# Order of the first loads, half-size V chunks, unnormed pool projection, paired FFN units and another buffer for y in an eight-core trunk kernel

## The chip, the cores and the metric

One Trainium2 chip; the program runs on all eight cores, each with its own rows and the same weights. The metric is the device time of the slowest core in microseconds (us). A run is called *slow* when one die (cores 0 to 3, or 4 to 7) is over 1% longer than the other at a lower clock of TensorE (PE), or when the run is over 1.5% above the fastest of its kernel. Only *fast* runs are compared.

## The reference

Each core carries 2048 prompt rows and 64 sample rows through four layers, in two groups `g` of 1024 prompt rows (the first with the sample rows). A layer is a token mixer and a gated FFN; even layers mix by gMLP, odd ones by pooling.

```python
for i in range(4):
    h = rmsnorm(x, norm_mix[i])
    if i % 2 == 0:                       # gMLP
        u, v = split(gelu(h @ w_in))     # 2048 columns each
        v = rmsnorm(v, g_v)              # per row, over 2048 columns
        y = (u * (masked_ws @ v + b_s)) @ w_out
    else:                                # pooling: trailing means over 2, 4, 8, 16 rows
        y = grouped(mean(h) - h, w_pool) * scale
    x = x + y
    h = rmsnorm(x, norm_ffn[i])
    x = x + (silu(causal_conv3(h @ w_gate)) * (h @ w_val)) @ w_down
y = rmsnorm(x, norm_final)
```

## The kernel before

The kernel records operations with the buffers that they read and write; a scheduler at build time then lays out one fixed order for each engine. So a load that the program text names first need not be first in its engine's queue. Weights come in 1 MB units through a ring of 64 KB per partition, issued by POOL (GpSimd); x, y and some of the constants are issued by SP (SyncE). DVE is VectorE, and PSUM the memory that matmuls write to, here handed out in banks of 512 columns. A group's rows are three tiles of up to 384.

```python
load_x(0, 0)                       # tile 0, two halves, SP
unit(("Uu", 0, 0, 0))              # first weight unit, POOL
...
for t in range(1, 3):
    load_x(0, t)                   # not gated by anything

# gMLP, V: one f32 buffer for a chunk of 128 rows x 2048 columns
for ci, (col0, nt, t) in enumerate(chunks):
    for half in range(2):
        ...                        # 16 matmuls into two PSUM banks
        rec(ACT, ... out=vsb.t[0:nt, half * 1024:(half + 1) * 1024] ... Gelu ...)
    rec(ACT, ... Square of all of vsb, sum into vs ...)
    rsqrt_col(vs, nt)              # twelve one-column operations, DVE
    rec(DVE, ... vb = vsb * rsqrt * g_v, 2048 columns ...)
    ...                            # spatial product: bias row, 16 matmuls from vb

# FFN
for u in range(6):
    wg = unit(("Wg", g, l, u)); wv = unit(("Wv", g, l, u))
    for t, (c0, n) in enumerate(TILES[g]):
        ...                        # gate and value matmuls, 4 pairs (u = 5: 2)

# end of a group
def final_tile(g, t):
    ...                            # DVE: xT = xT * scale * rstd, in place
    dma(SP, y_out ..., xT ...)     # two halves
# and then load_x(g + 1, t) into the same xT
```

Before a pooling layer all rows were normed (Ln and Exp on ScalarE, eight scalings on DVE), then projected, 1024 columns at a time over two PSUM banks.

Of the kernel before, what the change touches and what calls it, by code (L numbers as in the profile page):

```python
# [16 lines left out]
DV = 2048  # L17
# [101 lines left out]
class Recorder:  # L119
# [3 lines left out]
    def rec(self, eng, fn, reads=(), writes=(), cost=0.0, dsem=None, nbytes=0, tab=None, pt=()):  # L123
# [21 lines left out]
        for w in writes:  # L145
            for o in w.overl:
                if o.last_write is not None:
                    add(o.last_write, False)
                for t in o.reads:
                    add(t, False)  # L150
        deps.pop(op, None)
# [11 lines left out]
    def schedule(self, engines, window=160):  # L163
# [16 lines left out]
        dma_free = [0.0]  # L180
# [18 lines left out]
        def best(name):  # L199
# [8 lines left out]
            while i < L and n < window:  # L208
# [9 lines left out]
                if op.news:  # L218
                    (tile,) = op.news
                    if tile.pred is not None and tile.pred.b is None:  # L220
                        continue
                    p = place(tile, s, reserved)
                    if p is None:
                        for g_ in tile.groups:
                            reserved.update(g_)
                        continue
                    _, grp, t = p
                    if t > s:
                        reserved.update(grp)
                        s = t  # L230
# [8 lines left out]
        while remaining:  # L239
# [35 lines left out]
            if op.dsem is not None:  # L275
                b = max(s + c + 1.3, dma_free[0])
                dma_free[0] = b + op.nbytes / 230e3
                op.end = dma_free[0] + 0.8
            else:
                op.end = s + c  # L280
# [58 lines left out]
def build_program():  # L339
# [44 lines left out]
    with es:  # L384
# [42 lines left out]
        for i in range(2):  # L427
            vnb.append(alloc(f"vn{i}", [128, DV], BF16, off=o))
            o += 4096
        junk = alloc("junk", [128, DV], BF16, off=o)  # L430
# [9 lines left out]
        hS = alloc("hS", [128, KC, NSM], F32, off=M0 + 4 * NTMAX * 2, pieces=[((k,), k * NSM, (k + 1) * NSM) for k in range(KC)])  # L440
# [26 lines left out]
        vstat = [alloc(f"vstat{i}", [128, 8], F32) for i in range(2)]  # L467
        epsb = alloc("epsb", [128, 1], F32)
# [3 lines left out]
        vsb = alloc("vsb", [128, DV], F32, off=X0 + 8192, pieces=[(0, 0, 1024), (1, 1024, 2048)])  # L472
# [9 lines left out]
        gout = alloc("gout", [64, DV], F32, off=acc[0].off)  # L482
# [44 lines left out]
        def dma(eng, out, in_, reads=(), writes=(), dsem=None, nbytes=0, cost=None):  # L527
            if cost is None:
                cost = 0.9 if eng is POOL else 0.1
            return rec(eng, lambda e: e.dma_start(out=out, in_=in_), reads, writes, cost, dsem, nbytes)  # L530
# [15 lines left out]
        def load_unit(key):  # L546
# [5 lines left out]
            dma(POOL, buf.t[:, :, :].rearrange("p a b -> p (a b)"), sap, writes=buf.all, dsem=ring_sems[i % NRS], nbytes=128 * a * b * 4)  # L552
# [6 lines left out]
        def load_x(g, t):  # L559
            c0, n = TILES[g][t]  # L560
            o = xoff[(g, t)]
            src = x_in[128 * o:128 * (o + KC * n)].rearrange("(p k c) -> p k c", p=128, k=KC)
            for h in range(2):
                ks = slice(4 * h, 4 * h + 4)
                dma(SP, xT.t[:, ks, c0:c0 + n], src[:, ks, :], writes=[xT.r[(k, t)] for k in range(4 * h, 4 * h + 4)],
                    dsem=xsem[(t, h)], nbytes=128 * 4 * n * 4)
# [5 lines left out]
        def const_load(buf, out, src, eng=POOL):  # L572
            cs[id(buf)] = newdsem(f"d_c{len(cs)}")
            dma(eng, out, src, writes=buf.all, dsem=cs[id(buf)], nbytes=100000)

        load_x(0, 0)
        unit(("Uu", 0, 0, 0))
# [6 lines left out]
        def consts_late():  # L584
            const_load(pvf, pvf.t[:, :, :].rearrange("p a b -> p (a b)"), vec_f, SP)
            const_load(maskT, maskT.t[:], c_mask)
# [5 lines left out]
            od = newdsem("d_old")  # L592
            for j in range(2):
                dma(SP, pool_old[j], st_old[j], dsem=newdsem(f"d_old{j}"), nbytes=700000)
# [66 lines left out]
        def norm_pool_extra(g, t, l):  # L661
            c0, n = TILES[g][t]
            rs = rstd[t % 2]
            j = l // 2
            if t != 2:
                return
            if g == 0:
                for kc in range(KC):
                    rec(DVE, lambda e: e.scalar_tensor_tensor(out=hS.t[:, kc, :], in0=xT.t[:, kc, NP:NP + NSM],
                                                               scalar=pvd.t[:, kc, l:l + 1], in1=rs.t[:, 256:320], op0=ALU.mult, op1=ALU.mult),  # L670
                        reads=[xT.r[(kc, t)]] + rs.all + pvd.all, writes=[hS.r[(kc,)]], cost=dvec(NSM, True))
# [3 lines left out]
            else:  # L675
                for kc in range(KC):
                    rec(DVE, lambda e: e.scalar_tensor_tensor(out=hpp.t[:, kc, :], in0=xT.t[:, kc, NP - 15:NP],
                                                               scalar=pvd.t[:, kc, l:l + 1], in1=rs.t[:, 241:256], op0=ALU.mult, op1=ALU.mult),
                        reads=[xT.r[(kc, t)]] + rs.all + pvd.all, writes=hpp.all, cost=dvec(16, True))
                dma(SP, pool_prompt[j], hpp.t[:, :, :].rearrange("p a b -> p (a b)"), reads=hpp.all, dsem=hpp_sem, nbytes=62000)  # L680

        def proj_tile(g, t, mm_list):
            c0, n = TILES[g][t]
            for dc in range(KC):
# [3 lines left out]
                def f(e):  # L688
# [5 lines left out]
                    pt=[(bk, False)], reads=[xT.r[(dc, t)]], writes=[xT.r[(dc, t)]], cost=dvec(n))  # L694
                stat_add(g, t, dc)

        def rsqrt_col(vs, nt):
            def tiny(f):
                rec(DVE, f, reads=vs.all, writes=vs.all, cost=0.13)
            c = lambda i: vs.t[0:nt, i:i + 1]  # L700
            ci_ = lambda i: vs.t[0:nt, i:i + 1].bitcast(I32)
            tiny(lambda e: e.tensor_scalar(out=c(2), in0=c(0), scalar1=EPS, scalar2=None, op0=ALU.add))  # L702
            tiny(lambda e: e.tensor_scalar(out=ci_(3), in0=ci_(2), scalar1=1, scalar2=None, op0=ALU.logical_shift_right))
            tiny(lambda e: e.tensor_scalar(out=ci_(1), in0=ci_(3), scalar1=-1.0, scalar2=1597463007.0, op0=ALU.mult, op1=ALU.add))
            for _ in range(3):
                tiny(lambda e: e.scalar_tensor_tensor(out=c(4), in0=c(1), scalar=c(1), in1=c(2), op0=ALU.mult, op1=ALU.mult))
                tiny(lambda e: e.tensor_scalar(out=c(4), in0=c(4), scalar1=-0.5, scalar2=1.5, op0=ALU.mult, op1=ALU.add))
                tiny(lambda e: e.tensor_tensor(out=c(1), in0=c(1), in1=c(4), op=ALU.mult))
# [5 lines left out]
        def mixer_a(g, l, after_tile):  # L714
            j = l // 2
            dma(SP, gvb.t[:], g_v[j].partition_broadcast(128), writes=gvb.all, dsem=gv_sem, nbytes=1048576)
# [13 lines left out]
            for t, (c0, n) in enumerate(TILES[g]):  # L730
                for u in range(4):
# [17 lines left out]
            for ci, (col0, nt, t) in enumerate(chunks):  # L749
                vb = vnb[ci % 2]  # L750
                vs = vstat[ci % 2]
                for half in range(2):
                    bks = palloc(2, range(4), chain='v')

                    def mmv(e):
                        for q in range(2):
                            w = vu[2 * half + q]
                            for kc in range(KC):
# [5 lines left out]
                    rec(ACT, lambda e: e.activation(out=vsb.t[0:nt, half * 1024:(half + 1) * 1024], in_=pap(bks, 0, 1024)[0:nt, :], func=AF.Gelu_apprx_tanh),  # L764
                        pt=[(bks, False)], writes=[vsb.r[half]], cost=actc(1024), tab="gelu")
                rec(ACT, lambda e: e.activation(out=junk.t[0:nt, :], in_=vsb.t[0:nt, :], func=AF.Square, scale=float(DV) ** -0.5, accum_out=vs.t[0:nt, 0:1]),  # L766
                    reads=vsb.all, writes=junk.all + vs.all, cost=actc(2048) + 0.2)
                rsqrt_col(vs, nt)
                rec(DVE, lambda e: e.scalar_tensor_tensor(out=vb.t[0:nt, :], in0=vsb.t[0:nt, :], scalar=vs.t[0:nt, 1:2], in1=gvb.t[0:nt, :],  # L769
                                                          op0=ALU.mult, op1=ALU.mult),  # L770
                    reads=vsb.all + vs.all + gvb.all, writes=vb.all, cost=dvec(2048, True))
                if nt == NSM:
                    rec(DVE, lambda e: e.scalar_tensor_tensor(out=gout.t[:], in0=vsb.t[0:NSM, :], scalar=vs.t[0:NSM, 1:2], in1=gvb.t[0:NSM, :],
                                                              op0=ALU.mult, op1=ALU.mult),
                        reads=vsb.all + vs.all + gvb.all, writes=gout.all, cost=dvec(2048, True))
# [51 lines left out]
        def mixer_b_tile(g, l, t):  # L827
# [3 lines left out]
            for t, (c0, n) in [(t, TILES[g][t])]:  # L831
                cl = [c for c in range(8) if c // 3 == t]
                for c in cl:
                    zt = zb[c] if not (g == 0 and c == 7) else zlast[j]
                    ztile[c] = zt
                    bks = palloc(2)

                    def mmz(e):
                        for gi in range(4):
                            for cc in range(2):  # L840
                                i = e.matmul(pap(bks, gi * 256, (gi + 1) * 256), lhsT=hB.t[:, 2 * gi + cc, 2 + c * 128:2 + (c + 1) * 128],  # L841
                                             rhs=wp.t[:, 2 * gi + cc, :], start=(cc == 0), stop=(cc == 1))
                        return i
                    rec(PE, mmz, reads=wp.all + [hB.r[(kc, t)] for kc in range(KC)], pt=[(bks, True)], cost=mmc(8, 256))
# [339 lines left out]
```

## Time and profile before

| what | before |
|---|---|
| all runs, median | 3122.05 us (20 runs, 3052.05 to 3446.16) |
| PE busy, slowest core | 2895.5 us of 3078.8 |
| PE clock, mean of the cores | 0.945 to 0.966 |
| DVE, ScalarE (ACT), POOL busy | 49%, 39%, 15% |

The PE is the bound, so the kernel's time is its matmul work plus what it idles plus what it loses by running below full clock. The list of cores is the view to start from; its columns are span and mean clock:

```profile
core 0: 3052.7 us, clock 0.953
...
core 4: 3023.0 us, clock 0.965
core 5: 3015.3 us, clock 0.966
...
core 7: 3078.8 us, clock 0.945
```

Same program, same instructions, 64 us apart, and the longer the span, the lower the clock, but for cores 1 to 3, which lie within 4 us. Where this trace shows a clock of 0.8125, it lasts 159.5 to 161.5 us at a time: once on cores 0 to 3, twice on 6 and 7, never on 4 and 5. In the first of core 7 (629 to 791 us) matmuls of 384 columns start 197 ns apart, where they start 162 ns apart at clock 1.00 (800 to 900 us). Each costs 161 x (1 - 0.8125) = 30 us. Below I call these *0.81 stretches*, and take them out of stage lengths, since they hide what a change does.

### The profile page before, as it was taken

The numbers are of one execution on the slowest core, as the hardware profiler recorded it, in microseconds if no ns is written. First come the engines' busy times: TensorE is split into PE (matmuls) and PEld (weight loads), VectorE is DVE, ScalarE is ACT, GpSimd is POOL, SyncE is SP. The second block draws the span as 40 slices with busy tenths as digits, with TensorE's granted clock in tenths as the row PEclk, the third lists the DMA queues.
The fourth block names the chain that finished last, engine by engine and source line by source line (L and its number), as shares of the span: only waits on it lengthen the run. The fifth ranks groups of instructions, "written<-read, shape, count | busy, mean of one in ns | idle before, by whom it ended". The sixth has DMA issues, their size and how long they took to land.

```text
span 3078.8 us, 51559 instructions; the slowest of 8 cores (3015.3 to 3078.8 us)
## 1 busy us (share of the span) xinstructions
PE 2895.5 (94%) x18552; PEld 1806.7 (59%) x18552; DVE 1516.1 (49%) x2968; ACT 1186.0 (39%) x2209; POOL 471.4 (15%) x832
## 2 busy tenths in 40 slices
PE   1989999899999999989998999999999999999998
PEld 0545666555664566655565556666666556666665
DVE  1056663455314666355533356635663166635663
ACT  1433442533243344244324434424443334424541
POOL 1003221112210222212121021010002011011001
PEclk8999999888999999988899999998999999998999
DMA  9407441543344563263437435324453434424341
GB/s 190 73 6 124 67 73 33 91 65 57 56 72 66 96 94 49 45 104 60 63 80 158 69 59 98 56 41 83 70 97 65 80 55 83 71 41 84 58 74 55
DMA packets 49272, 227.76 MB, mean 74 GB/s; under 512 B 6240, under 2 KB 19168, under 8 KB 31456
## 3 DMA queue, kind: packets, MB, share of 16 engines
q0 software_dynamic: 32960, 193.75, 39.1%
q1 hardware_dynamic: 16064, 30.72, 3.4%
q8 instruction: 153, 2.51, 0.3%
q14 instruction: 95, 0.78, 0.1%
HBM read 406.32 MB, written 13.32 MB: 136 GB/s over the span
## 4 chain that ended last, share of the span: by engine, by line
PE 82%; DVE 7%; ACT 4%; issue 3%; DMA 3%; another core or an unknown queue 1%; DVEq 0%; SPq 0%; ACTq 0%
PE psum L690 26%; PE psum L923 22%; PE psum L930 21%; PE psum L739 7%; PE psum L888 2%; PE psum L759 2%; ACT junk L766 1%; DMA xT<-x_in 1%; DMA y_out<-xT 1%; DVE hB L653 1%; DVE vn_48 L769 1%; DVE vn_47 L769 1%; PE psum L841 1%; ACT vsb L764 1%
## 5 line engine op out<-in xcount | busy, mean ns | idle before, releaser
L693 DVE TENSOR_TENSOR xT<-psum,xT 128x384 f32<-128x384 f32 (+2 forms) x288 | 147.9, 522 | 483.5 <-PE psum L690 483.1
L947 DVE SCALAR_TENSOR_TENSOR cb_91<-psum,pvf,cb_91 128x384 f32<-128x384 f32 (+1 forms) x264 | 151.0, 572 | 68.7 <-ACT cb_91 L937 42.4
L947 DVE SCALAR_TENSOR_TENSOR cb_90<-psum,pvf,cb_90 128x384 f32<-128x384 f32 (+1 forms) x264 | 150.7, 571 | 65.6 <-ACT cb_90 L937 52.5
L947 DVE SCALAR_TENSOR_TENSOR cb_89<-psum,pvf,cb_89 128x384 f32<-128x384 f32 (+1 forms) x264 | 150.8, 571 | 63.1 <-ACT cb_89 L937 39.4
L947 DVE SCALAR_TENSOR_TENSOR cb_88<-psum,pvf,cb_88 128x384 f32<-128x384 f32 (+1 forms) x264 | 150.8, 571 | 55.7 <-ACT cb_88 L937 44.1
L602 ACT ACTIVATE sq_58<-xT 128x384 f32<-128x384 f32 (+2 forms) x126 | 62.4, 496 | 283.1 <-DVE xT L693 263.4
L602 ACT ACTIVATE sq_57<-xT 128x384 f32<-128x384 f32 (+2 forms) x126 | 62.4, 495 | 280.2 <-DVE xT L693 258.9
L653 DVE SCALAR_TENSOR_TENSOR hB<-xT,pvd,rstd_64 128x384 bf16<-128x384 f32 (+2 forms) x256 | 129.9, 579 | 67.1 <-ACT rstd_64 L645 67.1
L764 ACT ACTIVATE vsb<-psum 128x1024 f32<-128x1024 f32 (+1 forms) x68 | 66.4, 1021 | 230.8 <-DVE vn_47 L769 94.1
L743 ACT ACTIVATE UB<-psum 128x384 bf16<-128x384 f32 (+2 forms) x192 | 86.4, 466 | 108.4 <-PE psum L739 108.1
L937 ACT ACTIVATE cb_90<-psum,pvf 128x384 f32<-128x384 f32 (+2 forms) x132 | 84.4, 639 | 112.5 <-PE psum L923 110.1
L937 ACT ACTIVATE cb_88<-psum,pvf 128x384 f32<-128x384 f32 x132 | 84.5, 640 | 105.5 <-PE psum L923 103.4
L937 ACT ACTIVATE cb_91<-psum,pvf 128x384 f32<-128x384 f32 (+2 forms) x132 | 84.3, 639 | 101.6 <-PE psum L923 101.6
L937 ACT ACTIVATE cb_89<-psum,pvf 128x384 f32<-128x384 f32 x132 | 84.2, 638 | 91.0 <-PE psum L923 91.0
L702 DVE TENSOR_SCALAR vstat_81<-vstat_81 128x1 f32<-128x1 f32 (+1 forms) x18 | 2.7, 152 | 226.0 <-ACT junk L766 226.0
L954 POOL TENSOR_SCALAR stmp_84<-ASb,pvf 128x64 f32<-128x64 f32 x88 | 38.8, 440 | 479.2 <-ACT ASb L940 477.1
L960 DVE TENSOR_TENSOR mT<-cb_91,psum 128x384 bf16<-128x384 f32 (+2 forms) x132 | 68.4, 518 | 88.4 <-ACT cb_91 L959 71.0
L960 DVE TENSOR_TENSOR mT<-cb_89,psum 128x384 bf16<-128x384 f32 x132 | 68.4, 518 | 86.6 <-ACT cb_89 L959 60.4
L959 ACT ACTIVATE cb_90<-cb_90 128x384 f32<-128x384 f32 (+2 forms) x132 | 65.1, 493 | 88.3 <-DVE cb_90 L947 78.7
L959 ACT ACTIVATE cb_88<-cb_88 128x384 f32<-128x384 f32 x132 | 65.2, 494 | 81.5 <-DVE cb_88 L947 68.8
L960 DVE TENSOR_TENSOR mT<-cb_88,psum 128x384 bf16<-128x384 f32 x132 | 68.3, 517 | 51.9 <-ACT cb_88 L959 51.6
L960 DVE TENSOR_TENSOR mT<-cb_90,psum 128x384 bf16<-128x384 f32 (+2 forms) x132 | 68.3, 518 | 51.5 <-ACT cb_90 L959 50.5
(789 smaller groups left out, 6399.8 us busy)
## 6 DMA issues: line engine op xcount, KB each, us to landing
xT<-x_in SPq DMA_DIRECT2D x8, 768.0 KB, 7.2
y_out<-xT SPq DMA_DIRECT2D x8, 768.0 KB, 3.9
ASb<-st_conv SPq DMA_DIRECT2D x4, 1056.0 KB, 11.3
gvb<-g_v SPq DMA_DIRECT2D x4, 1024.0 KB, 11.4
pool_old<-st_old SPq DMA_DIRECT2D x2, 704.0 KB, 50.5
conv_sample<-cst SPq DMA_DIRECT2D x4, 352.0 KB, 7.1
xT<-x_in SPq DMA_DIRECT2D x2, 640.0 KB, 61.0
y_out<-xT SPq DMA_DIRECT2D x2, 640.0 KB, 8.3
```

What stands on the lines that cost most here:

```text
L602: rec(ACT, lambda e: e.activation(out=dst.t[:, 0:n], in_=xT.t[:, kc, c0:c0 + n], func=AF.Square), reads=[xT.r[(kc, t)]], writes=dst.all, c ...
L653: rec(eng, lambda e: e.scalar_tensor_tensor(out=hB.t[:, kc, 2 + c0:2 + c0 + n], in0=xT.t[:, kc, c0:c0 + n], scalar=pvd.t[:, kc, gidx:gidx ...
L690: ins = e.matmul(pap(bk, 0, n), lhsT=lt, rhs=rh, start=(i == 0), stop=(i == len(mms) - 1))
L693: rec(DVE, lambda e: e.tensor_tensor(out=xT.t[:, dc, c0:c0 + n], in0=pap(bk, 0, n), in1=xT.t[:, dc, c0:c0 + n], op=ALU.add), pt=[(bk, Fals ...
L739: i = e.matmul(pap(bk, 0, n), lhsT=ub.t[:, kc, e4 * 128:(e4 + 1) * 128], rhs=hB.t[:, kc, 2 + c0:2 + c0 + n], start=(kc == 0), stop=(kc == ...
L764: rec(ACT, lambda e: e.activation(out=vsb.t[0:nt, half * 1024:(half + 1) * 1024], in_=pap(bks, 0, 1024)[0:nt, :], func=AF.Gelu_apprx_tanh) ...
L923: i = e.matmul(pap(gb, 0, n + 2), lhsT=wg.t[:, kc, fs], rhs=hB.t[:, kc, c0:c0 + n + 2], start=(kc == 0), stop=(kc == KC - 1))
L930: i = e.matmul(pap(vb, 0, n), lhsT=wv.t[:, kc, fs], rhs=hB.t[:, kc, 2 + c0:2 + c0 + n], start=(kc == 0), stop=(kc == KC - 1))
L937: rec(ACT, lambda e: e.activation(out=cb.t[:, 0:n], in_=pap(gb, 2, 2 + n), func=AF.Identity, bias=sc(12 + l), scale=sc(3 * l + 2)), pt=[(g ...
L947: rec(DVE, lambda e: e.scalar_tensor_tensor(out=cb.t[:, 0:npr], in0=pap(gb, 2 - sh, 2 - sh + npr), scalar=sc(3 * l + 2 - sh), in1=cb.t[:, ...
L959: rec(ACT, lambda e: e.activation(out=cb.t[:, 0:n], in_=cb.t[:, 0:n], func=AF.Silu), reads=cw, writes=cw, cost=actc(n, False), tab="silu")
L960: rec(DVE, lambda e: e.tensor_tensor(out=mT.t[:, fc, c0:c0 + n], in0=cb.t[:, 0:n], in1=pap(vb, 0, n), op=ALU.mult), pt=[(vb, False)], read ...
```

## The change

Its intent has five parts: x ahead of the weights in the first loads; V of the gMLP in half chunks with three buffers; rows projected before the norm of a pooling layer, with the norm's factor applied where PSUM is copied out; the first two FFN units in pairs per tile, so that the norm of the next tile has twice the work to hide behind; and the final rows written to another buffer, so that at the turn, where the second group of rows follows the first, the next x need not wait for y to leave. The core of the diff (cuts marked by `...`):

```diff
-        load_x(0, 0)
-        unit(("Uu", 0, 0, 0))
+        xl0 = load_x(0, 0)
+        load_unit(("Uu", 0, 0, 0), behind=xl0[:1])
+        xl1 = load_x(0, 1, behind=xl0[1:])
+        load_unit(("Uu", 0, 0, 1))
+        xl2 = load_x(0, 2, behind=xl1[1:])
+        load_unit(("Uu", 0, 0, 2))
+        load_unit(("Uu", 0, 0, 3))
...
-                    rec(ACT, lambda e: e.activation(out=vsb.t[0:nt, half * 1024:(half + 1) * 1024], in_=pap(bks, 0, 1024)[0:nt, :], func=AF.Gelu_apprx_tanh),
+                    rec(ACT, lambda e: e.activation(out=vx.t[0:nt, :], in_=pap(bks, 0, 1024)[0:nt, :], func=AF.Gelu_apprx_tanh),
+                    ...   # vx = vh[(2 * ci + half) % 3]; square and scaling by halves as well
...
+                if xg is not None:   # beside the down projection in front of a pooling layer
+                    rec(ACT, lambda e: e.activation(out=hB.t[:, dc, 2 + c0:2 + c0 + np_], in_=xT.t[:, dc, c0:c0 + np_], func=AF.Copy, scale=pvd.t[:, dc, xg:xg + 1]),
...
-                    bks = palloc(2)          # projection z: 1024 columns, two banks
+                    for zh in range(2):
+                        bk = palloc()        # 512 columns, one bank
+                        ...
+                        rec(ACT, lambda e: e.activation(out=zt.t[:, zh, :], in_=pap(bk), func=AF.Copy, scale=rcol[t].t[:, ci:ci + 1]),
...
-            for u in range(6):
+            pairs = [(u, t) for t in range(3) for u in range(2)] + [(u, t) for u in range(2, 6) for t in range(3)]
+            for u, t in pairs:
...
-                rec(DVE, lambda e: e.scalar_tensor_tensor(out=xT.t[:, kc, c0:c0 + n], ...
+                rec(DVE, lambda e: e.scalar_tensor_tensor(out=yv(kc, kc + 1), ...     # yv: in mT
```

Two more edits are in the scheduler: its model of transfers now has a clock for each of the two queues and 300 GB/s (230 before), and when a tile must wait for PSUM it now reserves one group of banks, not all that would do.

## The prediction

> **What bounds the kernel now.** I read the page's busy shares and slices first, then the list of what TensorE (PE) waited for, then the busy times of chosen stretches, then the timeline and the DMA view of the first 100 us. All are of core 7, the slowest.
>
> ```profile
> PE 2895.5 (94%) x18552; PEld 1806.7 (59%) x18552; DVE 1516.1 (49%) x2968; ACT 1186.0 (39%) x2209; POOL 471.4 (15%) x832
> ...
> PE   1989999899999999989998999999999999999998
> ...
> PEclk8999999888999999988899999998999999998999
> ```
>
> PE is the bound: 94% busy, DVE only 49%. But slice 0 is nearly empty, and in several places the granted clock falls below full speed. So the change can only win what PE loses by idling or by running slowly; it removes almost no matmul. Its waits:
>
> ```profile
> PE psum L630 <- ACT sqb_60 L602: 31.9, 4, 15.4
> PE psum L923 <- DVE hB L653: 27.1, 5, 6.7
> PE psum L841 <- DVE cb_88 L947: 15.9, 2, 8.0
> PE psum L783 <- DVE vn_48 L769: 14.1, 7, 5.0
> PE psum L759 <- ACT vsb L764: 13.9, 13, 3.4
> ```
>
> L630 are the statistics of the first norm (they wait for x). L923 is the first FFN matmul after a pooling layer, waiting for normed rows. L841 is the pool projection. L759 and L783 are the gMLP V matmul and the spatial product after it. The stretches in which they lie (length; PE busy; PE's clock behind POOL's time):
>
> ```profile
> 0.00:142.00 142.00, 74.24 (x410) 42.16 (x411) 19.97 (x42) 40.66 (x74) 12.45 (x27) 0.88 0.68 130
> 142.00:262.00 120.00, 104.16 (x600) 52.01 (x598) 66.11 (x135) 39.86 (x45) 11.04 (x13) 0.93 0.31 50
> 522.00:642.00 120.00, 104.94 (x662) 67.11 (x661) 62.67 (x125) 56.17 (x94) 21.08 (x41) 0.82 0.49 80
> 1672.00:1712.00 40.00, 29.21 (x153) 15.01 (x152) 7.58 (x16) 23.83 (x42) 0.00 (x0) 0.83 0.44 125
> 629.00:790.00 161.00, 161.00 (x866) 93.92 (x864) 88.92 (x166) 62.69 (x128) 34.03 (x86) 0.81 0.46 69
> ```
>
> I count as lost: length minus busy times clock. Start (0 to 142): 142 - 74.2 x 0.88 = 77 us. First gMLP V stage: 120 - 104.2 x 0.93 = 23; the same sum for the other three V stages gives 16, 12 and 11, so 62 together. First pooling layer: 120 - 104.9 x 0.82 = 34; the other three give 28, 29 and 19, so 110. Turn from the first half of the rows to the second (1672): 40 - 29.2 x 0.83 = 16. Together 265 us. Plain FFN stretches are 100% busy at clock 1.00. The last row is different: no idle time, but clock 0.81 for 161 us, 30 us lost; core 7 has two such stretches, cores 4 and 5 none (3015 to 3023 us against 3079). That is the chip's doing, and makes a few tens of us of scatter even in fast runs.
>
> [...]in the DMA view of 42 to 66 us and the issues of 0 to 110 us:
>
> ```profile
> q0 software_dynamic: 515, 3.74, 89.8%
> q1 hardware_dynamic: 515, 0.64, 11.5%
> ...
> xT<-x_in SPq DMA_DIRECT2D x2, 640.0 KB, 61.0
> ```
>
> 515 packets each: the weights (q0) moved 3.74 MB, x (q1) 0.64 MB, 27 GB/s. Two x loads of 640 KB took 61 us to land.
> [...]The clock's low stretches here are 0.5 (219 us on core 7) and 0.8125[...].
> [...]
>
> **The change, part by part.**
> *First loads.* The aim is x before weights. But only weight unit 0 got the wait. The order of the changed kernel's POOL queue shows units 1, 2, 3, the spatial weights, and V units 4 and 5 issued at once, without a wait; unit 0 sixth, once the first half tile of x has landed. So 8 KB weight packets still run beside x. Worse, each x tile is now issued only when the one before has landed. My reconstruction: first tile landed at about 22 us (18.6 before, when small constant packets ran beside it; they are now later). Second tile (1.57 MB) from 22: about 34 GB/s beside weights, faster during 3 us of small packets; its second half lands at about 62 us (40.8 before), when the eight weight units (6.3 us each) are through. Third tile then has the engines alone: 1.31 MB at some 200 GB/s[...], so 72 us (77 before). PE gets 24 matmuls at 42 us, then 56 from 63 us, then from 75 us runs without stops. What is left then is about 160 matmuls of 384 columns and 128 of 320; at the 160 ns and 133 ns spacing of warm ones 43 us, plus 2 for warming. U ends at about 120 instead of 141.6: **-22 us**. With a real gate it could have been -50: 4.2 MB of x is 19 us at 225 GB/s, and the U work itself is 58 us.
>
> *gMLP V in half chunks.* The period before, from one chunk's second gelu to the next chunk's gelus:
>
> ```profile
> 148.80 1.02 ACT L764 ACTIVATE vsb<-psum 128x1024 f32<-128x1024 f32 x1 [2.43 <-PE psum L759]
> 149.91 1.91 ACT L766 ACTIVATE junk<-vsb 128x2048 bf16<-128x2048 f32 x1
> 152.02 0.15 DVE L702 TENSOR_SCALAR vstat_81<-vstat_81 128x1 f32<-128x1 f32 x1 [60.88 <-ACT junk L766]
> 155.34 2.35 DVE L769 SCALAR_TENSOR_TENSOR vn_47<-vsb,vstat_81,gvb 128x2048 bf16<-128x2048 f32 x1
> 157.84 1.94 ACT L764 ACTIVATE vsb<-psum 128x1024 f32<-128x1024 f32 x2 [5.93 <-DVE vn_47 L769]
> ```
>
> One V buffer makes this a ring: gelus 1.94, square 2.1, twelve one-column operations at 0.26 each 3.3, scaling 2.35, handoffs: 10 us, against PE's 4 x 1.73 = 6.9 us a chunk and 1.5 us of spatial product. With three half buffers only one gelu (1.02), half a square (1.3), thirteen small operations (3.5) and half the scaling (1.25) stay in the ring: 7.3 us with handoffs, below PE's 8.4. DVE then has 3.5 + 2.5 + 2.3 = 8.3 us a chunk, just under PE. Of 62 us I take about half: the waits (45 us) shrink to some 15, and the slow clock after them goes in part: **-33**.
>
> *Pool projection of unnormed rows, FFN in pairs.* Ln, Exp and eight norm operations (8 x 0.54 = 4.3 us) leave the way to the projection, 24 ScalarE copies a layer come in beside the down projection (3.5 us of PE per 0.5 us copy, hidden). The first FFN phase after pooling has 8 units of work per tile in place of 4 (2.9 us each), so the next tile's norm is covered: the waits of L923 (27 us) go. The 15.9 us at L841 are for a PSUM bank that DVE frees late, behind norm operations; one bank in place of two helps, but the DVE queue and the table loads stay, so half: 8. The half-speed clock around these gaps gives back some 15. **-50** of 110; the many 16 and 128 column matmuls of L888 stay.
>
> *Turn.* The last norm writes to another buffer, so new x no longer waits for y to leave: **-8** of 16.
>
> Sum -22 - 33 - 50 - 8 = **-113 us**. The fast runs before (3052, 3053, 3081) mean 3062, so fast runs of about 2949. The stated median, 3112, holds slow runs; I put the median of the changed kernel at **2975**, between 2949 and 3112 - 113 = 2999.
>
> **Rivals.** (1) The gate works as named, or x is less starved: start -50, fast runs near 2920. For: the intent. Against: the POOL order. (2) The gate backfires fully: the later second tile stalls PE and the start gains nothing; fast runs near 2970. (3) DVE becomes the bound of the V stages (8.3 of 8.4 us) and late bank frees keep the pooling gaps: V -15, pool -20, fast runs near 3000. For: L841 waits for DVE today. [...]
>
> **Range and chances.** One rival alone moves the result by 20 to 50 us, the clock by 30 to 60: 2915 to 3050. To miss 2% (61 us) two parts would have to fail: faster 0.93, same 0.06, slower 0.01.
>
> **What would show it.** Right: weight unit 1 ahead of unit 0 in the trace; second x tile landing near 60 us; U stage over at 110 to 130 us; V waits below 20 us; no FFN wait for hB above 3 us after pooling; PE busy 96 to 97%. Wrong: U over before 100 us (gate works) or after 135; projection waits above 6 us still there; idle time gone but clock lower, so that the span stays.

What no trace of this case shows is cut from it: a rule of the DMA queues, two of the clock, a figure for ScalarE's table loads, a fixed 2 us in the time of the third x tile, and a fourth rival, in which the change brought more 0.81 stretches. The sum of the parts came to the -113 us that it names, with those 2 us in it; without them the third tile would come at about 70 us, the start at -24 and the sum at -115.

The other figures can be set beside the trace of the kernel before, core 7. x alone moved at 207 GB/s from 2.3 to 7 us, and at 235 from 3 to 7; the 225 and the 200 are estimates near these. At clock 1.00, matmuls of 384 columns start 162 ns apart and those of 320 columns 136 (160 and 133 in the text). "Warming" stands for what PE did when it started again at 77.9 us: clock 0.50 and 320 ns apart until 81.5, then 1.00 and 162; the 2 us for it are an estimate. A table load of ScalarE took 1.28 us. What the half-speed clock gives back in V and in pooling is an estimate, too: in the first V stage a wait of 3.4 us ended at 159.0 and the clock was at 0.50 from 160.1 to 163.5; the first pooling layer has five such pieces, 37 us in all.

## The result

| | before | changed |
|---|---|---|
| all runs, median | 3122.05 us (20 runs) | 2947.17 us (10 runs, 2946.12 to 3130.7) |
| fast runs | 3052 to 3081 us | 2946 to 2949 us, and the profiled one 2977 us |
| ratio of fast runs | | 0.959, 95% interval 0.9557 to 0.9623 |

A ratio here is the mean time of one kernel's fast runs over that of the other's in the same rounds; it is not quite the ratio of two medians. Results are correct, and the change is faster. The page of the changed kernel, shares and slices as in the prediction:

```profile
PE 2847.5 (96%) x18576; PEld 1791.5 (60%) x18576; DVE 1489.7 (50%) x3134; ACT 1235.5 (42%) x2385; POOL 470.0 (16%) x832
...
PE   2999999999999999999996999999999999999998
...
PEclk8999999899999889989998999998999999998999
```

Only two slices are not at 9 or near it: the start and the turn (slice 21, counted from 0, which was 8 before). What PE waited for:

```profile
PE psum L649 <- ACT sqb_62 L621: 38.4, 4, 24.4
PE psum L649 <- ACT sqb_61 L621: 25.7, 2, 17.2
PE psum L649 <- ACT sqb_63 L621: 19.1, 1, 19.1
PE psum L838 <- DVE vn_47 L823: 8.5, 7, 4.6
PE psum L912 <- ACT mT L901: 7.3, 2, 3.6
PE psum L989 <- ACT mT L901: 5.4, 2, 2.7
```

L649 are the first norm's statistics (L630 before): they wait for x. At the start they waited 62 us before and 58 now; the 24.4 us in the first line is new and lies at the turn. The FFN's waits for normed rows (L923 before, 27.1 us) and the projection's waits for a bank (L841 before, 15.9 us) are gone. In the V stages only L838, the bias row ahead of the spatial product, still waits (16 us in all, where the V stages' waits were 45). Waits for ScalarE's copy of the projection (ACT L901, before L845) went from 4.4 to 12.7 us. The stretches that answer to those shown of before (length; PE, weight loads, DVE, ACT, POOL busy; PE's clock):

```profile
0.00:128.00 128.00, 69.76 (x409) 41.26 (x410) 19.96 (x42) 42.39 (x75) 12.94 (x28) 0.93 0.73 145
128.00:235.00 107.00, 102.42 (x614) 52.93 (x613) 66.42 (x156) 43.01 (x63) 9.68 (x13) 0.95 0.40 68
493.00:610.00 117.00, 113.36 (x748) 73.54 (x746) 67.93 (x158) 61.66 (x116) 18.10 (x34) 0.88 0.38 69
1560.00:1600.00 40.00, 15.59 (x92) 9.33 (x90) 1.97 (x4) 7.42 (x12) 3.94 (x6) 0.70 0.85 178
```

Start and V are shorter, the pooling layer has a better clock (0.88 for 0.82), the turn is worse: 15.6 us of work in 40 us, against 29.2 before.

To tell the parts apart I cut every core's trace at its first V matmul and at the first down-projection matmul of each of the eight FFNs (D00 is layer 0 of the first group, D13 layer 3 of the second), took out 1 - 0.8125 of the time at 0.81, and took the median of the cores. All from the profiled runs, in us:

```
stage      holds             before   changed  difference
0-V        start, U           141.2    128.1     -13.1
V-D00      V                  320.0    306.5     -13.5
D00-D01    pooling            302.5    286.4     -16.1
D01-D02    V                  453.8    443.6     -10.2
D02-D03    pooling            295.6    284.8     -10.8
D03-D10    turn, V            443.0    445.4      +2.4
D10-D11    pooling            278.5    271.7      -6.8
D11-D12    V                  419.8    411.0      -8.8
D12-D13    pooling            275.0    271.7      -3.3
D13-end                        87.9     88.4      +0.5
sum                          3017.3   2937.6     -79.7
```

So the kernel gained **80 us**. The fast runs differ by some 125; the other 45 I put down to 0.81 stretches, of which the profiled run before has 0, 30 or 61 us by core. The changed kernel's profiled run has one of 161.2 us on cores 2 and 3; that run took 2977 us, and the other fast ones of the same kernel 2946 to 2949. This is seen on other chips too: on two of the three chips of the experiments, all fast runs of the kernel before were at 3026 to 3039 us with a clock of 0.96 to 0.97 on nearly all cores (on the third: 3082 and 3105). From 3030 there to 2947 here is 83 us, across chips, and near the 80 of the table.

### The profile page after: what moved, and what is told of

Read it like the earlier page. It is cut to its first block, busy times and chain, and to the rows that moved or that the text cites. A ratio compares the mean times of both kernels' runs of the same rounds, so it can differ in the third digit from the quotient of the medians.

```text
span 2975.1 us, 52581 instructions; the slowest of 8 cores (2925.4 to 2975.1 us)
## 1 busy us (share of the span) xinstructions
PE 2847.5 (96%) x18576; PEld 1791.5 (60%) x18576; DVE 1489.7 (50%) x3134; ACT 1235.5 (42%) x2385; POOL 470.0 (16%) x832
## 4 chain that ended last, share of the span: by engine, by line
PE 87%; DMA 4%; DVE 3%; issue 3%; ACT 2%; DVEq 0%; SPq 0%; ACTq 0%
PE psum L720 27%; PE psum L989 22%; PE psum L982 22%; PE psum L786 7%; PE psum L809 4%; DMA xT<-x_in 4%; PE psum L945 2%; PE psum L649 1%; PE psum L897 1%; DVE vn_47 L823 1%; PE psum L841 0%; DVE vn_48 L823 0%; DVE nwt L743 0%; DVE UB L845 0%; DMA gmlp_v<-gout 0%
## 5 line engine op out<-in xcount | busy, mean ns | idle before, releaser
L727 ACT ACTIVATE hB<-xT,pvd 128x384 bf16<-128x384 f32 (+1 forms) x96 | 55.4, 577 | 186.7 <-DVE xT L723 168.2
L996 ACT ACTIVATE cb_99<-psum,pvf 128x384 f32<-128x384 f32 (+2 forms) x132 | 84.4, 640 | 108.4 <-PE psum L982 108.3
L996 ACT ACTIVATE cb_96<-psum,pvf 128x384 f32<-128x384 f32 (+2 forms) x132 | 84.5, 640 | 102.6 <-PE psum L982 100.6
L996 ACT ACTIVATE cb_98<-psum,pvf 128x384 f32<-128x384 f32 (+2 forms) x132 | 84.7, 641 | 96.7 <-PE psum L982 94.3
L672 DVE SCALAR_TENSOR_TENSOR hB<-xT,pvd,rstd_66 128x384 bf16<-128x384 f32 (+2 forms) x192 | 101.5, 599 | 46.0 <-ACT rstd_66 L664 41.7
L996 ACT ACTIVATE cb_97<-psum,pvf 128x384 f32<-128x384 f32 (+2 forms) x132 | 84.3, 639 | 92.8 <-PE psum L982 90.4
L1019 DVE TENSOR_TENSOR mT<-cb_99,psum 128x384 bf16<-128x384 f32 (+2 forms) x132 | 68.2, 517 | 73.9 <-ACT cb_99 L1018 59.3
L818 DVE TENSOR_TENSOR vstat_83<-vstat_83 128x1 f32<-128x1 f32 (+1 forms) x18 | 2.8, 156 | 195.7 <-ACT junk L816 195.7
L1019 DVE TENSOR_TENSOR mT<-cb_97,psum 128x384 bf16<-128x384 f32 (+2 forms) x132 | 68.2, 517 | 64.4 <-ACT cb_97 L1018 48.7
L1018 ACT ACTIVATE cb_98<-cb_98 128x384 f32<-128x384 f32 (+2 forms) x132 | 65.0, 492 | 70.6 <-DVE cb_98 L1006 60.8
L1018 ACT ACTIVATE cb_96<-cb_96 128x384 f32<-128x384 f32 (+2 forms) x132 | 65.1, 493 | 68.5 <-DVE cb_96 L1006 58.5
L1018 ACT ACTIVATE cb_97<-cb_97 128x384 f32<-128x384 f32 (+2 forms) x132 | 64.7, 490 | 63.3 <-DVE cb_97 L1006 55.3
L1019 DVE TENSOR_TENSOR mT<-cb_98,psum 128x384 bf16<-128x384 f32 (+2 forms) x132 | 68.1, 516 | 44.9 <-ACT cb_98 L1018 42.8
## 6 DMA issues: line engine op xcount, KB each, us to landing
xT<-x_in SPq DMA_DIRECT2D x8, 768.0 KB, 18.4
ASb<-st_conv SPq DMA_DIRECT2D x4, 1056.0 KB, 10.8
```

The lines of the kernel that those rows point to most:

```text
L672: rec(eng, lambda e: e.scalar_tensor_tensor(out=hB.t[:, kc, 2 + c0:2 + c0 + n], in0=xT.t[:, kc, c0:c0 + n], scalar=pvd.t[:, kc, gidx:gidx ...
L996: rec(ACT, lambda e: e.activation(out=cb.t[:, 0:n], in_=pap(gb, 2, 2 + n), func=AF.Identity, bias=sc(12 + l), scale=sc(3 * l + 2)), pt=[(g ...
L1018: rec(ACT, lambda e: e.activation(out=cb.t[:, 0:n], in_=cb.t[:, 0:n], func=AF.Silu), reads=cw, writes=cw, cost=actc(n, False), tab="silu")
L1019: rec(DVE, lambda e: e.tensor_tensor(out=mT.t[:, fc, c0:c0 + n], in0=cb.t[:, 0:n], in1=pap(vb, 0, n), op=ALU.mult), pt=[(vb, False)], read ...
```

## The experiments

Twelve kernels, each correct. "Net" is the sum of the table above for that kernel. The kernel before was run beside each set; the changed kernel was not, so comparisons with it are across chips, and a net is one profiled execution: stages that an edit doesn't touch differ by up to some 5 us (D02 to D03 is 283.9 to 288.5 in the kernels that keep its form).

**1. First loads as before.**

```diff
-        xl0 = load_x(0, 0)
-        load_unit(("Uu", 0, 0, 0), behind=xl0[:1])
-        ...
+        load_x(0, 0)
+        unit(("Uu", 0, 0, 0))
+        ...   # the other x tiles, constants and U order as before, too
```

> The changed kernel with the first loads and the order of the first U units as before. Theory A (the parts add up along TensorE's path; the stretches at clock 0.81 are a separate matter): only the start moves, the first V matmul comes at 139 to 143 us again instead of 128, and the fast runs are 13 us longer, about 2960 us. Rival B (the later start is only hidden time, since V units and late constants bound the stage): the end of the first gMLP layer moves by less than 5 us. Rival C (the order of the first loads is what removed the 0.81 stretches): fast runs at 2990 or 3020 us.

Measured: net 2942.1; fast runs 2949.9 and 2952.8 us. First V matmul at 137.4 (changed: 128.1), but from there to the first down projection 298.7 against 306.5. So rival B holds: the start's 9 us are mostly given back in the next stage. This part of the change is worth 1.5 us by these two stages and 4 to 5 by the net and the fast runs. In PE time the two stages differ by idle 2.1 against 6.5 us and loss of clock (half of the busy time at half speed) 0.0 against 4.3. The changed kernel's PE order there:

```profile
157.32 1.89 PE L809 MATMUL psum<-w_114,hB 128*128 128x512 bf16 x8
159.15 0.40 PE L838 MATMUL psum<-brow,onesb 1*128 1x512 bf16 x4
159.47 1.07 PE L841 MATMUL psum<-wsT,vn_47 128*128 128x128 bf16 x16
163.09 0.61 PE L838 MATMUL psum<-brow,onesb 1*128 1x512 bf16 x4 [2.55 <-DVE UB L845]
```

The first spatial product stands 31 us after the first V matmul, where its rows had been ready for 16 us (and the last bias row for 17), and then two come in a row, so the second waits for DVE.

**2. V in whole chunks.** The V loop, its buffer and its one-column operations as before, the rest changed.

```diff
-        vh = [alloc("vh2", [128, 1024], F32, off=o)]
-        ...   # three half buffers
+        vsb = alloc("vsb", [128, DV], F32, off=X0 + 8192, pieces=[(0, 0, 1024), (1, 1024, 2048)])
```

> The changed kernel with one whole V buffer per chunk as before, the square and the scaling in one piece. Theory A: the four gMLP passes get their waits back, 9 to 14 us each, together about 40 us: fast runs near 2985 us, the waits of the V and bias-row matmuls back from 17 to about 45 us. Rival: if VectorE was the bound in both forms (8.3 us of work a chunk against 8.4 us of TensorE), less than 15 us come back. [...]

Measured: net 2979.3; fast runs 2983.6 and 2981.9 us. The four V stages are 12.5, 8.5, 10.0 and 8.8 us longer: 39.8, as theory A has it. The waits of V behind the one V buffer are back (L818 is V; it waits for ScalarE to copy PSUM out, which waits for the buffer):

```profile
PE psum L843 <- DVE vn L828: 15.4, 9, 2.6
PE psum L818 <- ACT vsb L823: 14.2, 11, 3.4
```

The ring of the prediction is cut as described. In the changed kernel ScalarE's rows read:

```profile
145.50 1.02 ACT L814 ACTIVATE vh_93<-psum 128x1024 f32<-128x1024 f32 x1 [0.85 <-PE psum L809]
146.61 1.06 ACT L816 ACTIVATE junk<-vh_93 128x1024 bf16<-128x1024 f32 x1
147.58 0.19 ACT L816 ACTIVATION_READ_ACCUMULATOR junk<-vh_93 128x1 f32 x1
149.63 1.02 ACT L814 ACTIVATE vh_94<-psum 128x1024 f32<-128x1024 f32 x1 [1.87 <-DVE vn_48 L823]
```

The first gelu waits for PE, no longer for a buffer; the next waits 1.87 us for one, where before it was 5.93.

**3. Projection of normed rows.** The norm ahead of the projection, as before; the projection still goes by one-bank halves.

```diff
-                        rec(ACT, lambda e: e.activation(out=zt.t[:, zh, :], in_=pap(bk), func=AF.Copy, scale=rcol[t].t[:, ci:ci + 1]),
+                        rec(ACT, lambda e: e.activation(out=zt.t[:, zh, :], in_=pap(bk), func=AF.Copy),
...
-                proj_tile(g, t, mm_list, l + 1 if l % 2 == 0 else None)
+                proj_tile(g, t, mm_list)
```

> The changed kernel with the pool projection reading normed rows again (Ln, Exp and norm before it), but still in halves of one PSUM bank, and with the FFN units in pairs. Theory A: the two parts of the pooling change share the 38 us that the four pooling layers gained; the projection's half of it is about 15 to 25 us: fast runs 2961 to 2971 us. Rival: the FFN pairs alone did it, and less than 8 us come back. Rival 2: the norm chain returns whole to the path at each of the twelve tiles, 40 us or more.

Measured: net 2937.4, the changed kernel 2937.6; fast runs 2945.2 and 2947.4 us. The four pooling stages sum to 1109.5 against 1114.6. So the rival holds: this part, the largest in the diff, is worth nothing once the pairs are there.

**4. FFN units one by one.**

```diff
-            pairs = [(u, t) for t in range(3) for u in range(2)] + [(u, t) for u in range(2, 6) for t in range(3)]
+            pairs = [(u, t) for u in range(6) for t in range(3)]
```

> The changed kernel with the FFN units in their old order (all three tiles of a unit before the next unit). Theory A: after each pooling layer the first FFN matmul of the last tile waits for the norm again, 3 to 7 us each, 20 us together with the slow clock after them: fast runs near 2965 us without 0.81 stretches. [...]

Measured: net 2960.6; four runs, all fast, 2967.3 to 2968.6 us. The pooling stages sum to 1134.6, 20 us more, as theory A has it, and the wait is back:

```profile
PE psum L982 <- DVE hB L672: 25.3, 6, 6.8
```

None of its cores has an 0.81 stretch, on a chip whose fast runs of before (3082 and 3105 us) have clocks down to 0.937. So the waits behind a pooling layer came back here without the stretches. None of experiments 1 to 4 brought them back.

**5. The gate as its text reads.** All POOL loads of the first layer wait for the third x tile's first half, units 0 and 1 for the first halves of tiles 0 and 1; the norm's scales are loaded ahead of x.

```diff
+            if eng is POOL and gate_now and not behind:
+                behind = gate_now
...
+        const_load(pvd, pvd.t[:, :, :].rearrange("p a b -> p (a b)"), vec_d, SP)
         xl0 = load_x(0, 0)
         load_unit(("Uu", 0, 0, 0), behind=xl0[:1])
         xl1 = load_x(0, 1, behind=xl0[1:])
-        load_unit(("Uu", 0, 0, 1))
+        load_unit(("Uu", 0, 0, 1), behind=xl1[:1])
         xl2 = load_x(0, 2, behind=xl1[1:])
+        gate_now.extend(xl2[:1])
```

> The changed kernel with the gates as its author seems to have meant them: norm scales first, weight unit 0 behind the first half of the first x tile, unit 1 behind the second tile's first half, all other early loads of the same queue behind the third tile's. Theory A (x is starved by 8 KB weight packets because only one of the weight loads waits): second x tile landed by 22 to 30 us instead of 68, third by 40 us instead of 74, first V matmul at 85 to 95 us instead of 128, fast runs near 2908 to 2915 us. Rival B (the weights are what the start waits for, and the gate only moves the wait from x to weights): first V matmul not before 115 us.

Measured: net 2901.0; fast runs 2909 to 2913 us. V begins at 89.7 us, 38 us earlier than in the changed kernel. The reason is in the issues. The changed kernel's POOL queue and, from its list of transfers (size, us from issue to landing), two of its loads:

```profile
1.55 0.70 POOL L544 DMA_DIRECT2D w_110<-wts  x1 [0.87 <-POOLq L349]
2.25 0.54 POOL L544 DMA_DIRECT2D w_111<-wts  x1
2.77 0.55 POOL L544 DMA_DIRECT2D w_112<-wts  x1
...
6.92 0.54 POOL L544 DMA_DIRECT2D w_109<-wts  x1 [0.46 <-issue]
```

```profile
xT<-x_in SPq DMA_DIRECT2D x4, 768.0 KB, 20.9
...
w_109<-wts POOLq DMA_DIRECT2D x1, 1024.0 KB, 47.2
```

Only w_109, unit 0, stood behind x; the units that the text names later went first, and the built order gives unit 0 its first matmul only at 97.6 us (unit 1, w_110, at 44.5). So the gate held back a load that nothing waited for, and eight weight loads, all issued by 8.5 us, shared the engines with x: from 28 to 62 us the weights' queue moved 936 packets, 5.02 MB, and SP's 938, but only 1.41 MB. SP's queue shows what became of x:

```profile
22.59 46.34 SPq L544 DMA_DIRECT2D xT<-x_in  x4
```

That is tile 1 issued at 22.6 and tile 2 not before 68, each behind the last. PE waits for it: its matmuls stand behind the statistics of tile 1 until 44 us and of tile 1's second half until 69. With the gate on every load theory A holds: the same transfers take 10.5 us in the median, tile 1 has landed at 25.0 us and tile 2 at 38.0, and SP and POOL read:

```profile
1.51 25.23 SPq L548 DMA_DIRECT2D xT<-x_in  x6
```

```profile
9.01 0.70 POOL L548 DMA_DIRECT2D w<-wts  x1 [8.32 <-DMA xT<-x_in]
23.55 0.53 POOL L548 DMA_DIRECT2D w<-wts  x1 [13.85 <-DMA xT<-x_in]
36.84 1.05 POOL L548 DMA_DIRECT2D w<-wts  x2 [12.76 <-DMA xT<-x_in]
```

**6. All of x first, then weights.** As 5, with the x tiles issued at once and every weight behind the last of them.

```diff
-        xl1 = load_x(0, 1, behind=xl0[1:])
-        xl2 = load_x(0, 2, behind=xl1[1:])
+        xl1 = load_x(0, 1)
+        xl2 = load_x(0, 2)
+        gate_now.extend(xl2[1:])
```

> The changed kernel with norm scales and all of x first, every weight load behind the last half tile of x. x is 4.2 MB, about 19 us at the 225 GB/s that x had alone in the first 7 us, so landed at 21 to 23 us; weight unit 0 about 8 us later, near 30 us, when TensorE starts and then has work without stops: 58 us of U work and 3 for warming, first V matmul at 92 to 97 us. Against the interleaved gate this tells whether a simple order is as good: within 8 us of it. If the fixed time of a weight load (issue to first packet, about 5 us) counts each time, it is later, beyond 100 us.

(The 5 us are 5.4 in the kernel before: w_101 was issued at 1.55 us, and the first packet of the weights' queue started at 6.96. The 225 GB/s and the warming are the estimates of the prediction.)

Measured: net 2906.3, V at 96.1 us; fast runs 2914 to 2918. So weights and x in turn, as the change meant it, are 5 to 6 us better than x alone first.

**7 and 8. The turn as before.** y is written from x in place, so the next x waits for y. In the second kernel y's stores are also cut into the same 768-byte runs as in the changed kernel.

```diff
-                rec(DVE, lambda e: e.scalar_tensor_tensor(out=yv(kc, kc + 1), ...
+                rec(DVE, lambda e: e.scalar_tensor_tensor(out=xT.t[:, kc, c0:c0 + n], ...
```

> The changed kernel with the last norm written in place and y stored from x's own buffer, as before, so that new x waits for y again. Theory A (the change made the turn worse: stores with 768 B runs and x loads take turns with 8 KB weight packets on one queue, and TensorE waited 24 us for the second x tile): the turn takes 10 to 15 us less, fast runs near 2934 us. Rival (the turn's wait comes from something else, as the order of the statistics on TensorE): no change within 4 us, or longer by the wait for y.

> As the one with y stored in place, but each store cut in two column halves, so that its runs are 768 B (640 and 512 B for the last tiles) as in the changed kernel, and x still waits for y. If the size of the runs is what made the turn longer (packets counted, not bytes, beside weights): the turn is as long as in the changed kernel or longer, fast runs 2945 us or more. If it is the early issue of x between the y stores: as fast as the in-place form, near 2934 us.

Measured: net 2924.9 and 2928.1 (the first's profile with 0.81 stretches on the second die, taken out here; its fast runs 2941.3 and 2942.6; the second's 2934.6 to 2941.3). The stage of the turn is 439.9 and 440.3 long, against 445.4, so removing the buffer *helps*, and the size of the runs is not the cause. SP's queue of the changed kernel, then of the first of these two:

```profile
1551.35 0.37 SPq L544 DMA_DIRECT2D y_out<-mT  x1
1551.78 1.59 SPq L544 DMA_DIRECT2D xT<-x_in  x1
1553.49 25.48 SPq L544 DMA_DIRECT2D y_out<-mT  x1
1579.01 8.93 SPq L544 DMA_DIRECT2D xT<-x_in  x1
```

```profile
1556.09 2.50 SPq L544 DMA_DIRECT2D y_out<-xT  x2
1588.05 7.00 SPq L544 DMA_DIRECT2D xT<-x_in  x2
```

With the other buffer, the first half of the second x tile goes out at once, between the halves of y, and PE waits for it until it has landed, at 1590.75 us, 39 us after its issue:

```profile
1563.94 3.15 PE L720 MATMUL psum<-mT,w_214 128*128 128x320 bf16 x22
1591.50 0.48 PE L649 MATMUL psum<-sqb_62,meanb 128*128 128x384 bf16 x1 [24.41 <-ACT sqb_62 L621]
```

The issue of y's second half took 25.48 us, with two transfers of its queue under way in front of it; that these held it is inferred. The early issue bought little: from 1555 to 1586 us SP's queue moved 648 packets of 768 bytes beside 650 of the weights' queue, 582 of them of 8192 bytes. Set against the end of the down projection in front of it, this half of x lands 21.5 us later in the changed kernel (median of the cores; 18.0 to 24.1), 24.2 and 24.7 in experiments 7 and 8, and 26.0 before. So x is not later than it was. What differs is what PE's order puts between that end and the statistics of this tile: no matmul of the new group in the changed kernel, 40 in experiments 7 and 8, 144 in the kernel before (143 on two cores). PE's order in the kernel before, and in experiment 7:

```profile
1676.42 1.89 PE L759 MATMUL psum<-w_212,hB 128*128 128x512 bf16 x8
1681.92 0.32 PE L630 MATMUL psum<-sqb_60,meanb 128*128 128x384 bf16 x1 [3.61 <-ACT sqb_60 L602]
```

```profile
1574.46 4.06 PE L786 MATMUL psum<-hB,w 128*128 128x384 bf16 x24
1597.06 1.30 PE L649 MATMUL psum<-sqb,meanb 128*128 128x384 bf16 x3 [18.54 <-ACT sqb L621]
```

In the 60 us after that end PE idles 23.9 us in the changed kernel, 18.4 and 18.8 in experiments 7 and 8, and 10.3 before (medians of the cores). That is the loss: the stage should have become 10 us shorter through V's halves, and was 2.4 longer, so the turn cost 12.4, and of these undoing the buffer gives 5.5 back. Why the scheduler laid the order out so I did not test: its transfer model changed in the same diff, and y now lies in the memory that holds U of the next group. No run undoes the model alone.

Both kernels also have 3.6 to 4.0 us less in each of the two later pooling stages. There PE's order is the same and so are its waits; what differs is how many half-speed pieces of 3.4 us the clock dealt out (17.1 us in the median core of experiment 7 in place of 23.9).

**9. Before, with the pairs alone.**

```diff
-            for u in range(6):
+            for u, t in [(u, t) for t in range(3) for u in range(2)] + [(u, t) for u in range(2, 6) for t in range(3)]:
```

> The kernel before, with nothing changed but the order of the FFN's gate and value units: the first two units of each tile in pairs. Theory A (the pairs alone cover the norm of the next tile behind a pooling layer, whatever form the projection has): the four stages that hold a pooling layer shrink by some 21 us together (they were 302.5, 295.6, 278.5 and 275.0), net total near 2996 us, and no FFN matmul waits over 4 us for normed rows. Rival (the pairs only pay together with the unnormed projection and its one-bank halves, which make the layer's end early enough): under 10 us, net total above 3007. On a chip where the kernel before has stretches at clock 0.81 in its fast runs they show here too (30 us each) if the pooling stages' matmul order is not what sets them off.

Measured: net 2987.7; fast runs 2993.6 to 2995.6 us beside 3026 to 3031 of before, ratio 0.9892 (0.9875 to 0.9909). The pooling stages are 294.3, 289.8, 272.7 and 267.6: 27.2 us less, theory A and more. (In all it is 1.1%.) PE's waits have no FFN wait for rows any more, but still those for a bank:

```profile
PE psum L841 <- DVE cb L947: 21.4, 3, 8.3
```

No core has an 0.81 stretch, but neither have the runs of before on this chip, so that part says nothing.

**10. The changed kernel without pairs and without the unnormed projection.**

> The changed kernel with both the projection of unnormed rows and the FFN pairs undone. Without the pairs alone it stood at 2960.6 us net, without the unnormed projection alone at 2937.4, as the changed kernel itself (2937.6). Theory B (the unnormed projection is worth something only where the pairs don't already cover the wait: the two are redundant): 2970 to 2978 net, the four pooling stages back near 300, 293, 278 and 275. Rival (the projection is worth nothing in either case, and the 15 us of the pooling stages' gain that no single undo took away come from what both variants keep, the one-bank halves of the projection and the scheduler's new way to keep banks free): 2958 to 2964 net.

The edit is that of 3 and 4 together. Measured: net 2956.7; fast runs 2964.9 to 2967.6 us. Theory B wanted 2970 to 2978, and falls: without the pairs, too, the unnormed projection is worth nothing (2960.6 with it, 2956.7 without). The pooling stages sum to 1133.1, still 18.5 under before, with 23 us of FFN waits back:

```profile
PE psum L971 <- DVE hB L672: 23.1, 6, 6.8
PE psum L901 <- ACT mT L890: 7.1, 2, 3.5
```

What is missing in its list is the wait for a bank, 15.9 us before. All that this kernel keeps of the pooling part are the one-bank halves of the projection and the scheduler's way to reserve banks. So one of the two, or both, freed the bank, unless another part that stays did; no run parts them.

**11. A better version: gate as intended, turn as before.** The edits of 5 and 7.

> The changed kernel with every early weight load behind x (as the run with the gate as intended, 2901.0 us net) and with the turn as it was before (y written from x in place; that alone took 5.5 us off the turn and 3.7 each off the two later pooling stages, 12.7 in all). If the two are independent: 2888 net, fast runs 2893 to 2902. If the turn's gain was scatter of the schedule, it stays at 2901 and fast runs near 2911. Correct results expected.

Measured: net 2887.4; fast runs 2894.2, 2894.3, 2898.3 and 2900.9 us beside 3026 to 3031, ratio 0.9571 (0.9552 to 0.959). The gains add up as expected (2888). By its fast runs it beats the changed kernel, across chips, by about 50 us and the one before, on a chip where that had no 0.81 stretches, by 131.

**12. The same, with the four bias rows in one transfer.**

```diff
-            for q in range(4):
-                dma(POOL, brow.t[32 * q:32 * q + 1, :], b_big[j, q:q + 1, :], writes=brow.all, dsem=ws_sems[1], nbytes=2048)
+            dma(POOL, brow.t[0:97:32, :], b_big[j], writes=brow.all, dsem=ws_sems[1], nbytes=8192)
```

> The same, with the four bias rows of the spatial product loaded by one transfer in place of four that each wait for the one before. In the run with the gate as intended the fourth was issued at 118 us and the first spatial product came at 122.7, 33 us after the first V matmul at 89.7. If the bias rows hold it back: the first spatial product comes some 22 us after V begins, and the stage from V to the first down projection falls from 305.9 to about 299, total 5 to 8 us under the run beside it. If the static order of the matmuls, laid out at build time, keeps it late, or DVE is what the V stage waits for: within 2 us of the run beside it.

Measured: net 2885.4; fast runs 2899.9 and 2900.2 us (two slow ones). The first spatial product comes at 107.3 us in place of 121.4, so the chain of four small loads did hold it back, by the order made for it. But the stage from V to the first down projection is only 2.0 shorter (304.1 for 306.1): the clock's loss went from 4.0 to 1.7 us, the idle time only from 6.7 to 5.9. Neither expectation holds as put: the mechanism is real, and worth little. The runs show no difference in time.

## Why the prediction was right or wrong

The time, 2975, was close to the measured 2947, and inside the range; the sum behind it was not as good. It had 113 us for the parts, and they brought 80. The fast runs were predicted at 2949 and came at 2946 to 2949 all the same, because some 45 us of 0.81 stretches went as well. So the mark was hit in part by luck: a gain that was not in the sum filled the gap in it. That is **the fourth rival turned round**: it was to bring more of them. Why they were there before and are rarer now stays open: no single undo brought them back, and the same kernel before is free of them on other chips.

**First loads: -22 predicted, -13 measured in their stage, 1.5 to 5 in the end.** The reading that only unit 0 was gated, and so rival 1 would not come, was right. Mis-sized was the step "its second half lands at about 62 us": it landed at 68.0 (67.2 to 68.9 by core). The norm's scales also came late, at 28.7 us (a 48 KB load, 26.6 us in flight), but PE still waited for x, not for them, at 44 and 69 us. What the working left out altogether was the stage behind: a U stage that ends 9 us earlier met a V stage that was 8 us longer (experiment 1). The estimate that a real gate could give -50 was near: from 141.2 to 89.7 is 51.5 (experiment 5). (x is 4.46 MB by the prediction's own tiles, not 4.2, so 20 us and not 19.)

**V in halves: -33 predicted, about -40 measured** (experiment 2), with the mechanism as told: one gelu, half a square and half a scaling in the ring. The term that was too small is "I take about half". In the first V stage PE's idle time went from 17.0 to 6.5 us and the loss of clock from 6.0 to 4.3; in the last from 9.5 to 3.1 and from 2.6 to 0.0. Rival 3, DVE as the bound, did not come.

**Pooling: -50 predicted, -37 measured** (-16.1, -10.8, -6.8, -3.3), and by other parts than I had put first. The FFN waits of 27 us went, as predicted, and it was the pairs that did it: 27 us alone on the kernel before (experiment 9), 20 in the pooling stages on top of the others (experiment 4). The step that failed is the first: "Ln, Exp and eight norm operations leave the way to the projection". They do leave, and nothing ended earlier for it (experiments 3 and 10), for they were not on that way: before, the projection (L841) waited 15.9 us for banks and never for normed rows. Nor do these norm operations explain the late bank: with them back, in experiments 3 and 10, the projection waits for nothing. The 15.9 us of bank waits went in full, where I had taken half; the "half-speed clock around these gaps" gave back less than the 15 that I took. In the third pooling stage (D10 to D11) idle time fell from 11.4 to 3.8 us, but the clock's loss rose from 10.6 to 11.9: the clock was at half for 23.9 us, in pieces of 3.4 and 6.8, with two gaps of PE in the stage, of 2.7 and 1.2 us (core 3). What lowered it there was not tested.

**Turn: -8 predicted, +12 measured.** The step that failed is "so new x no longer waits for y to leave". It is issued some 35 us earlier and lands only 4.5 us earlier (21.5 for 26.0 after the down projection), beside y in its own queue and weights in the other: from 1555 to 1586 us SP's queue moved 648 packets and the weights' 650, but 0.50 MB against 4.77. And PE, which before had 144 matmuls of the new group to do in the meantime, now has none: its idle time at the turn went from 10.3 to 23.9 us. The prediction had looked at the buffer alone, at no transfer of the turn and not at PE's order there.

## What to carry to other kernels

A gate on a load only works if the scheduler cannot send the others ahead of it, so read the issuing queue of the built kernel, not the text: here the difference was 38 us. Ahead of a new buffer that lets a load start early, look at what shares its queue and its engines at that moment, and at how much work the built order puts in front of the first matmul that needs it. When several parts aim at the same wait, undo them one at a time and together: the largest part of this change was worth nothing, with or without the reordering of one loop. And take the clock's stretches out, core by core, before you say what a change has gained.
